# Splitting the first x load at 4 KB instead of 16 KB per partition

## Chip, cores, metric

One core of one Trainium2 chip. The metric is device time in microseconds (us); the kernel before has a median of 84.38 us (three runs, 84.36 to 84.47). All runs quoted are fast runs, with a granted clock of 1.00.

## Reference

```python
x, y: float32 [1024, 4096]
def reference(x, y, axis):          # axis = -1
    return np.sum(np.abs(x - y), axis=axis).astype(np.float32)
```

33.55 MB are read and 4 KB written. Each of the 128 partitions takes eight rows of x and y, 16 KB a row.

## The kernel before

Four rows of x go to `xa`, four of y to `yb`, the next three of x to `xb`; later rows of y reuse `yb` when VectorE has consumed it. VectorE subtracts, ScalarE takes the absolute value and sums along the row. `s_first` counts the first three transfers, each worth 16: one for each DMA engine. Every partition of a transfer is one contiguous run in memory; below, "a 16 KB row" and the like mean such a run. Each of the 16 DMA engines carries 8 of the 128. The last row is cut into five pieces.

```python
PIECES = [1728, 1024, 640, 384, 320]
...
    for r in (slice(0, 1), slice(1, H)):            # 16 KB, then 48 KB a partition
        put(lambda: nc.sync.dma_start(out=xa[:, r, :], in_=xr[:, r, :]).then_inc(s_first, 16), before="Drain")
    put(lambda: nc.scalar.dma_start(out=yb, in_=yr[:, 0:H, :]).then_inc(s_first, 16))
    put(lambda: nc.sync.dma_start(out=xb[:, 0:H - 1, :], in_=xr[:, H:K - 1, :]).then_inc(s_xb, 16))
    for k in range(H - 1):
        put(lambda: nc.sync.wait_ge(s_sub, k + 1))
        put(lambda: nc.sync.dma_start(out=yb[:, k, :], in_=yr[:, H + k, :]).then_inc(s_row[k], 16))
    ...                                             # the last row, in pieces, x and y by turns
    for k in range(H):
        sub(xa[:, k, :], yb[:, k, :], [(s_first, 48)] if k == 0 else [])
        absum(xa[:, k, :], ro[:, k:k + 1], s_act)
    sub(xb[:, 0, :], yb[:, 0, :], [(s_xb, 16), (s_row[0], 16)])     # "the fifth subtraction"
    ...
```

## Time and profile before

| | before |
|---|---|
| median time | 84.38 us |
| span in the profile | 82.8 us |
| VectorE busy, ScalarE busy | 36.4 us, 31.5 us |
| share of the 16 DMA engines' span | 95.7% |
| first subtraction starts | 41.14 us |
| idle before the fifth subtraction | 2.02 us |
| last reduction starts | 80.82 us |

The transfers fill the whole span; each compute engine is idle for over half of it. (Times of single packets in the prediction are 0.03 to 0.04 us early throughout: its first packet at 0.97 us is at 1.01 us from the start of the span, its last at 79.88 is at 79.92. Below they are counted from the start of the span.)

### The profile page before, as it was taken

The page shows a single profiled execution, that of the slowest core. Times are in us where ns is not written, and L with a number is a line of the kernel's source. Part 1 is how long each engine was busy: PE and PEld are TensorE (multiplying, and loading weights), DVE is VectorE, ACT ScalarE, POOL GpSimd, SP SyncE. Part 2 cuts the span into 40 slices and gives each one's busy share as a digit, 9 for nine tenths or more (in the row PEclk, how much of TensorE's full clock was granted, in tenths as well). Part 3 has the DMA queues.
Part 4 walks back from the last instruction along what each step waited for, and adds up shares of the span by engine and source line. Part 5 has one row for each costly group of instructions (what it writes and reads, how often), then busy time and mean ns, then how long its engine had stood idle before and what let it go on. Part 6 is the DMA issues. An engine that isn't in the chain of part 4 may idle for free.

```text
span 82.8 us, 104 instructions
## 1 busy us (share of the span) xinstructions
DVE 36.4 (44%) x16; ACT 31.5 (38%) x27; POOL 0.2 (0%) x4
## 2 busy tenths in 40 slices
DVE  0000000000000000000199999999279898999772
ACT  2400000000000000000000988979690599999990
POOL 0000000000000000000000000000000000000000
DMA  5992999989999999998888999859999999999950
GB/s 127 404 807 103 538 538 435 451 388 451 435 451 435 419 467 419 404 451 380 380 380 380 451 617 451 380 253 404 475 388 467 419 404 406 427 413 412 401 195 2
DMA packets 2592, 33.56 MB, mean 405 GB/s; under 512 B 416, under 2 KB 928, under 8 KB 1696
## 3 DMA queue, kind: packets, MB, share of 16 engines
q1 hardware_dynamic: 2448, 25.17, 72.3%
q10 hardware_dynamic: 144, 8.39, 23.4%
HBM read 33.55 MB, written 0.00 MB: 405 GB/s over the span
## 4 chain that ended last, share of the span: by engine, by line
DMA 63%; DVE 22%; SPq 10%; issue 1%
DMA yb_rows<-in_y_dram 63%; DVE xa_rows L128 21%; SPq L116 6%; SPq L119 4%; DVE last_piece L162 1%; DVE ro_sums L164 1%
## 5 line engine op out<-in xcount | busy, mean ns | idle before, releaser
L128 DVE TENSOR_TENSOR xa_rows<-xa_rows,yb_rows 128x4096 f32<-128x4096 f32 x4 | 17.4, 4420 | 41.1 <-DMA yb_rows<-in_y_dram 41.1
L133 ACT ACTIVATE xa_rows<-xa_rows 128x4096 f32<-128x4096 f32 x4 | 14.5, 3617 | 44.5 <-DVE xa_rows L128 44.5
L128 DVE TENSOR_TENSOR xb_rows<-xb_rows,yb_rows 128x2048 f32<-128x2048 f32 (+5 forms) x9 | 17.9, 2015 | 3.5 <-DMA yb_rows<-in_y_dram 3.5
L133 ACT ACTIVATE xb_rows<-xb_rows 128x2048 f32<-128x2048 f32 (+5 forms) x9 | 15.1, 1681 | 3.0 <-DVE xb_rows L128 2.9
L133 ACT ACT_TABLE_LOAD x1 | 1.3, 1283 | 1.7 <-PEq L186 1.7
L133 ACT ACTIVATION_READ_ACCUMULATOR xb_rows<-xb_rows 128x1 f32 x9 | 1.7, 186 | 0.0
L133 ACT ACTIVATION_READ_ACCUMULATOR xa_rows<-xa_rows 128x1 f32 x4 | 0.7, 186 | 0.0
L162 DVE TENSOR_TENSOR last_piece<-xb_rows,yb_rows 128x320 f32<-128x320 f32 x1 | 0.5, 492 | 0.3 <-DMA yb_rows<-in_y_dram 0.3
L164 DVE TENSOR_REDUCE ro_sums<-last_piece 128x1 f32<-128x324 f32 x1 | 0.5, 491 | 0.0
L156 DVE TENSOR_REDUCE ro_sums<-half_sums 128x2 f32<-128x4 f32 x1 | 0.1, 150 | 0.0
L186 POOL MEMSET const-bfloat16-1.0<- 128x1 bf16 x1 | 0.1, 101 | 0.0
L186 POOL MEMSET const-uint8-127<- 128x1 uint8 x1 | 0.1, 101 | 0.0
L186 POOL MEMSET const-float32-0.0<- 128x1 f32 x1 | 0.1, 98 | 0.2 <-issue 0.2
L186 POOL MEMSET const-float32-1.0<- 128x1 f32 x1 | 0.1, 98 | 0.0
## 6 DMA issues: line engine op xcount, KB each, us to landing
xa_rows<-in_x_dram SPq DMA_DIRECT2D x1, 6144.0 KB, 36.9
xb_rows<-in_x_dram SPq DMA_DIRECT2D x1, 6144.0 KB, 54.4
yb_rows<-in_y_dram SPq DMA_DIRECT2D x3, 2048.0 KB, 15.4
xa_rows<-in_x_dram SPq DMA_DIRECT2D x1, 2048.0 KB, 17.0
xb_rows<-in_x_dram SPq DMA_DIRECT2D x1, 864.0 KB, 17.7
yb_rows<-in_y_dram SPq DMA_DIRECT2D x1, 864.0 KB, 15.8
xb_rows<-in_x_dram SPq DMA_DIRECT2D x1, 512.0 KB, 16.6
yb_rows<-in_y_dram SPq DMA_DIRECT2D x1, 512.0 KB, 17.4
```

The source lines that it names most:

```text
L116: put(lambda: nc.sync.dma_start(out=xb[:, H - 1, c], in_=xr[:, K - 1, c]).then_inc(s_piece[i], 16))
L119: put(lambda: nc.sync.dma_start(out=yb[:, H - 1, c], in_=yr[:, K - 1, c]).then_inc(s_piece[i], 16))
L128: put(lambda: nc.vector.tensor_sub(out=tx, in0=tx, in1=ty).then_inc(s_sub, 1))
L133: put(lambda: nc.scalar.activation(tx, tx, ABS, accum_out=to).then_inc(sem, 1))
L156: put(lambda: nc.vector.reduce_sum(out=ro[:, K - 3:K - 1], in_=half, axis=AX).then_inc(s_end, 1))
L162: put(lambda: nc.vector.tensor_sub(out=last[:, n_part:n_part + w], in0=tx, in1=ty).then_inc(s_end, 1))
L164: put(lambda: nc.vector.reduce_sum(out=ro[:, K - 1:K], in_=last, axis=AX, apply_absolute_value=True).then_inc(s_end, 1))
L186: nc = _bacc.Bacc("TRN2", target_bir_lowering=False, num_devices=1)
```

## The change

Same bytes, same number of transfers and waits; the cut in the first 64 KB of x per partition moves from 16 to 4 KB. A smaller first transfer might get the stream going sooner.

```diff
-    for r in (slice(0, 1), slice(1, H)):
-        put(lambda: nc.sync.dma_start(out=xa[:, r, :], in_=xr[:, r, :]).then_inc(s_first, 16), before="Drain")
+    fa, fx = xa.rearrange("p k c -> p (k c)"), xr.rearrange("p k c -> p (k c)")
+    for c in (slice(0, 1024), slice(1024, H * C)):
+        put(lambda: nc.sync.dma_start(out=fa[:, c], in_=fx[:, c]).then_inc(s_first, 16), before="Drain")
```

## The prediction

> **What bounds the kernel now.** I read the page first (engine shares, the 40 slices, the DMA queues), then the waits, then the DMA view cut into stretches, and last the order in time around 58 to 66 us.
>
> ```profile
> DVE 36.4 (44%) x16; ACT 31.5 (38%) x27; POOL 0.2 (0%) x4
> ...
> DMA  5992999989999999998888999859999999999950
> ...
> q1 hardware_dynamic: 2448, 25.17, 72.3%
> q10 hardware_dynamic: 144, 8.39, 23.4%
> ```
>
> No compute engine is half busy. The two DMA queues together hold 72.3 + 23.4 = 95.7% of the 16 engines' span, which is 0.957 x 82.8 = 79.2 us. q10 is the single 8 MB load of y issued by ScalarE (128 rows of 64 KB): 0.234 x 82.8 x 16 / 128 = 2.42 us a row, or 65,536 B / 2.42 us = 27.1 GB/s an engine and 433 GB/s for sixteen. The dips in the slices (2, 5) come from counting a long packet where it starts; in the single packet records I find no engine idle between its first row at 0.97 us and the last at 79.88 us.
>
> ```profile
> DVE xa_rows L128 <- DMA yb_rows<-in_y_dram: 41.1, 1, 41.1
> DVE xb_rows L128 <- DMA yb_rows<-in_y_dram: 3.5, 6, 2.0
> ACT xb_rows L133 <- DVE xb_rows L128: 2.9, 2, 2.7
> ```
>
> VectorE starts only when one semaphore has counted three transfers: x first (16 KB a partition), x second (48 KB) and y (64 KB). The profile names y, but by the packet records the last of y's 16 counts was written at 36.9 us and the last of the second x transfer at 40.7 us, so x came last. This matters for the change. Until then 16.78 MB must land in any order; spread over their durations, the packets had moved 16.9 MB by 40.7 us. So almost nothing that is not needed was moved before the start.
>
> ```profile
> 0.00:3.00 3.00, 0.00 (x0) 1.28 (x1) 0.20 (x4) 1.00 0.72 213
> 3.00:41.00 38.00, 0.00 (x0) 0.00 (x0) 0.00 (x0) 1.00 1.03 445
> 41.00:60.50 19.50, 17.43 (x4) 13.02 (x7) 0.00 (x0) 1.00 0.95 411
> 60.50:70.00 9.50, 8.92 (x3) 6.77 (x5) 0.00 (x0) 1.00 0.98 420
> 70.00:80.00 10.00, 9.02 (x7) 9.78 (x14) 0.00 (x0) 1.00 0.99 399
> ```
>
> Last column: GB/s. Only the first 3 us are poor. A straight line through the bytes moved (3.556 MB by 10 us at 434 GB/s) meets zero at 10 - 8.19 = 1.8 us, although the first packet starts at 0.97 us: 0.83 us is lost in warming up. The first row of each engine took 0.8 to 1.68 us where later 16 KB rows take 0.611 us.
>
> ```profile
> 58.60 3.62 ACT L133 ACTIVATE xa_rows<-xa_rows 128x4096 f32<-128x4096 f32 x1 [0.62 <-DVE xa_rows L128]
> ...
> 60.59 4.42 DVE L128 TENSOR_TENSOR xb_rows<-xb_rows,yb_rows 128x4096 f32<-128x4096 f32 x1 [2.02 <-DMA yb_rows<-in_y_dram]
> ...
> 65.05 3.62 ACT L133 ACTIVATE xb_rows<-xb_rows 128x4096 f32<-128x4096 f32 x1 [2.73 <-DVE xb_rows L128]
> 65.38 2.29 DVE L128 TENSOR_TENSOR xb_rows<-xb_rows,yb_rows 128x2048 f32<-128x2048 f32 x1 [0.36 <-DMA yb_rows<-in_y_dram]
> ```
>
> Here the fifth subtraction waits 2.02 us for its row of y. The start of VectorE at 41.14 us therefore has 2.02 us of slack. Beyond it slack is short: ScalarE runs from 65.05 to 80.67 us with 0.2 us of gaps, and the last reduction, at 80.82 us, needs its sums. I put the free delay at 2.02 + 0.2 + 0.15 = about 2.35 us.
>
> **What the Trainium skill says.** "DMA: Bandwidth & Descriptors", section "Queues, rings and completion order": each DMA engine takes turns between the queues it has work for, a packet at a time. The trace agrees on the turns (16 KB x rows alternate with 64 KB y rows from about 5 us) but here a packet is one row, up to 64 KB, where the page gives 9 to 17 descriptors as typical. So the size of a row sets the share of each queue, which is what the change alters. Section "Where 436 GB/s comes from" of that page: the port ceiling is 435 GB/s. The trace shows 433 to 435 GB/s in most single microseconds from 4 us to 54 us, so the stream is at the ceiling. Section "Latency and other measured facts": a first byte comes about 0.6 us after issue on these queues; here the first row starts 0.60 us after its issuing instruction ended (0.97 against 0.376 us).
>
> **The change part by part.** The bytes, the number of DMA instructions and the number of rows (8 + 8 an engine) stay. Compute instructions and waits stay.
>
> 1. Cost a row. From 0.611 us for 16 KB and 2.418 us for 64 KB: (2.418 - 0.611) / 49,152 B gives 27.2 GB/s, and a constant of 0.611 - 16,384 / 27.2e3 = about 0.009 us. The same 16 rows pay the same constant, and the two x transfers together take 16 x 0.009 + 524,288 / 27.2e3 = 19.4 us an engine, before and after. Change: 0.0 us.
>
> 2. The start. If the first row of each engine is slow because the pipeline passes it on only when whole, a 4 KB row (0.16 us by the line above) saves 0.611 - 0.16 = 0.45 us of the 0.83 us. If it is a fixed latency, it saves nothing. I can't tell which from one size, and take a third: -0.15 us. This moves the whole stream, hence the end, one for one.
>
> 3. Running dry. The eight 4 KB rows last 8 x 0.16 = 1.3 us, so to 2.3 us or later. The second transfer is issued at 0.42 to 0.85 us, so its rows can start at 0.85 + 0.6 = 1.45 us. No gap: 0.0 us.
>
> 4. The turns. Before, y's first rows start at 4.86 to 6.12 us, after 5 to 7 rows of x. Then y gets 64 KB for each 16 or 48 KB of x and finishes first. Afterwards x rows of 60 KB face y rows of 64 KB, and both should end almost together near 40.5 us. If y starts after at most two 60 KB rows, its eighth row still goes before any row of xb (the next x load, 48 KB rows), and VectorE starts at 41.0 us as before. For each further x row that gets ahead of y's first, one xb row of 49,152 / 27.2e3 + 0.009 = 1.8 us slips in before y's last, on that engine. The semaphore waits for the slowest engine.
>
> Sum: -0.15 us with the start of VectorE unmoved, so 84.38 - 0.15 = about 84.25 us; the small chance of 4 going wrong lifts my number to 84.3 us.
>
> **The rivals.**
> (a) Faster, through a quicker first row. For: the slow first rows; the change looks made for it. Against: some engines began 0.4 us later than others, yet their second rows all start within 2.18 to 2.65 us, which looks like a latency that does not depend on the row. At best 84.38 - 0.45 = 83.9 us.
> (b) y pushed behind, so that xb rows intrude. For: y is issued at 1.26 us, and with the same 0.97 us to its first row it should have been ready at about 2.2 to 2.7 us, but it ran only 2.4 to 3.9 us later: engines had committed to some five more x rows. If they commit by number of rows, not bytes, and the 4 KB rows are over by then, five rows of 60 KB could go ahead. Against: at 2.2 to 2.7 us most of the 4 KB rows should still be in work, and they would fill that commitment. One intruding row (1.8 us) is inside the 2.35 us of slack; two (3.6 us) cost about 1.3 us: 85.6 us; three (5.4 us) cost 3.1 us: 87.4 us. A shift in order moves no bytes, so the stream would stay full and VectorE with ScalarE would become the bound.
> (c) Hidden altogether: the stream is full at both ends, nothing moves, 84.4 us. This is near my own number.
>
> **Range and chances.** Most of the weight lies between (a) at 83.9 and (c) at 84.4. I give (b) with two or more intruding rows about 15%, about half of it with three or more, which alone gives slower by 2% (above 86.07 us). Faster by 2% means 82.7 us, which would need 1.7 us off the stream; the whole warm-up is 0.83 us. So the chances are 0.01 faster, 0.92 same, 0.07 slower. The range, leaning to the slow side: 83.9 to 85.2 us.
>
> **What the profile after should show.** Step 2: the straight line through the bytes meets zero at 1.4 to 1.8 us; last row of data at 79.4 to 79.9 us. Step 3: no idle engine between 2 and 4 us. Step 4: VectorE starts between 40.6 and 43 us, and the 2 us gap before the fifth subtraction is still there or partly used. Under (b) VectorE starts at 44.5 us or later, that gap is gone, the stream still ends near 79.9 us, and the end is set by VectorE and ScalarE. The prediction would be wrong if long rows ran below 27 GB/s an engine, if an engine ran dry after its 4 KB rows, or if y waited behind many 60 KB rows.

## The result, and the profile after

84.61 us median (six runs, 84.53 to 84.88) beside 84.42 us (six runs, 84.33 to 84.58) for the kernel before. Ratio 1.0025, 95% interval 1.0008 to 1.0043. A ratio here is the mean time of one kernel's fast runs over that of the other's in the same rounds, so not quite the ratio of the medians. The loss of about 0.2 us is small but outside the noise, and the prediction had expected a gain of 0.15 us.

Waits of the changed kernel (us in total, times, longest us):

```profile
DVE xa_rows L130 <- DMA yb_rows<-in_y_dram: 42.8, 1, 42.8
DVE xb_rows L130 <- DMA yb_rows<-in_y_dram: 1.8, 5, 0.4
```

VectorE now starts 1.65 us later, and 1.7 us of its later waits are gone. In order of time (start, us), the changed kernel:

```profile
42.79 17.43 DVE L130 TENSOR_TENSOR xa_rows<-xa_rows,yb_rows 128x4096 f32<-128x4096 f32 x4 [42.79 <-DMA yb_rows<-in_y_dram]
...
60.66 4.43 DVE L130 TENSOR_TENSOR xb_rows<-xb_rows,yb_rows 128x4096 f32<-128x4096 f32 x1 [0.44 <-DMA yb_rows<-in_y_dram]
...
80.41 0.49 DVE L164 TENSOR_TENSOR last_piece<-xb_rows,yb_rows 128x320 f32<-128x320 f32 x1 [0.32 <-DMA yb_rows<-in_y_dram]
```

and the last subtraction of the kernel before:

```profile
80.29 0.49 DVE L162 TENSOR_TENSOR last_piece<-xb_rows,yb_rows 128x320 f32<-128x320 f32 x1 [0.28 <-DMA yb_rows<-in_y_dram]
```

The later start is used up in the gap before the fifth subtraction (2.02 us before, 0.44 us now). In both kernels the last subtraction waits for its transfer, so the stream still sets the end, and it comes 0.12 us later.

Why VectorE starts later is seen in the DMA view, cut to 33 to 41 us (queue, packets, MB, share; a packet is counted where it starts). q10 carries y. Kernel before:

```profile
q1 hardware_dynamic: 85, 3.39, 98.0%
q10 hardware_dynamic: 16, 0.00, 0.1%
```

Changed kernel:

```profile
q10 hardware_dynamic: 41, 2.10, 60.6%
q1 hardware_dynamic: 48, 1.77, 51.2%
```

Before, all of y's rows had started by 33 us (the last ends at 35.14 us); only its 16 counts (4-byte writes to the semaphore, one per engine) are there. Afterwards 32 of y's 128 rows are still to start. From 41.05 to 42.8 us the changed kernel shows

```profile
q1 hardware_dynamic: 16, 0.79, 103.7%
q10 hardware_dynamic: 7, 0.00, 0.2%
```

y's last data row ended at 40.83 us, but seven of its counts are written only after 41.05 us (42.22 to 42.42). Each is behind a 48 KB row of `xb` that is not needed yet: every engine had started its first one at 40.40 to 40.84 us (they are in the 33 to 41 us view), and the sixteen in this view are the second ones. The start of y's rows explains the seven. Changed kernel, 4.0 to 7.3 us and then 7.3 to 8.0 us, q10 alone:

```profile
q10 hardware_dynamic: 9, 0.59, 41.2%
```

```profile
q10 hardware_dynamic: 7, 0.46, 151.1%
```

Nine engines begin y after one 60 KB row of x (5.27 to 5.66 us), seven after two (7.47 to 7.69 us). The queues take turns, row by row, and the count takes a turn of its own. With y behind one x row: x1 y1 ... x8 y8, count of x, count of y, xb1. With y behind two: x1 x2 y1 ... x8 y7, count of x, y8, xb1, count of y. One xb row, 1.82 us, lies between the last y row and its count. The records do not name the engine, so that the seven are the same seven is inferred: from the equal numbers, here and in the runs below, and from the times, since in order of time the seven counts follow the seven starts by 34.71 to 34.76 us each, and the nine follow theirs by 35.16 to 35.19 us. The kernel before already showed the count's own turn: y's last row ended at 35.14 us, the last count came at 36.95 us, one 48 KB row of x later. There it cost nothing, as that row was needed too.

Last, the end of the stream, 79.94 to 80.2 us; kernel before, then changed kernel:

```profile
DMA packets 0, 0.00 MB, mean 0 GB/s; under 512 B 0, under 2 KB 0, under 8 KB 0
```

```profile
DMA packets 3, 0.00 MB, mean 10 GB/s; under 512 B 1, under 2 KB 3, under 8 KB 3
```

One engine is still on its last rows. The average of the 16 last counts hardly moved in this pair of profiles (79.74 before, 79.73 after); the latest of them did (79.91 before, 80.04 after).

### The profile page after: what moved, and what is told of

It reads as the page before. It is cut to its first block, busy times and chain, and to the rows that moved or that the text cites. A ratio compares the mean times of both kernels' runs of the same rounds, so it can differ in the third digit from the quotient of the medians.

```text
span 82.9 us, 104 instructions
## 1 busy us (share of the span) xinstructions
DVE 36.4 (44%) x16; ACT 31.6 (38%) x27; POOL 0.2 (0%) x4
## 4 chain that ended last, share of the span: by engine, by line
DMA 65%; DVE 22%; SPq 9%; issue 1%
DMA yb_rows<-in_y_dram 65%; DVE xa_rows L130 21%; SPq L118 6%; SPq L121 2%; DVE last_piece L164 1%; DVE ro_sums L166 1%
## 5 line engine op out<-in xcount | busy, mean ns | idle before, releaser
L130 DVE TENSOR_TENSOR xa_rows<-xa_rows,yb_rows 128x4096 f32<-128x4096 f32 x4 | 17.4, 4419 | 42.8 <-DMA yb_rows<-in_y_dram 42.8
```

What stands on the lines that cost most here:

```text
L130: put(lambda: nc.vector.tensor_sub(out=tx, in0=tx, in1=ty).then_inc(s_sub, 1))
```

## The experiments

Three questions: does the later start of VectorE cost anything, what decides when y begins, and what costs the 0.2 us? All runs compare with the kernel before on the same chip. "Last count" is when the last of the 16 engines completes the last piece of y; "mean" is the average of the 16. Both, like the two columns before them, come from the one profiled execution of each run. The span ends 2.82 to 2.90 us after the last count in every run but delay_4096 and y_after_first, where ScalarE ends later: otherwise the last count decides the time.

| run | first x load | median us | ratio (95%) | VectorE starts | gap before fifth | mean / last count |
|---|---|---|---|---|---|---|
| before | 16, 48 | 84.38 | | 41.14 | 2.02 | 79.74 / 79.91 |
| changed | 4, 60 | 84.61 | 1.0025 (1.0008 to 1.0043) | 42.79 | 0.44 | 79.73 / 80.04 |
| delay_1500 | 16, 48 | 84.37 | 1.0002 (0.9987 to 1.0017) | 42.59 | 0.39 | 79.73 / 79.85 |
| delay_4096 | 16, 48 | 86.01 | 1.0200 (1.0184 to 1.0215) | 45.46 | 0 | 79.69 / 79.94 |
| y_after_first | 4, 60 | 85.10 | 1.0073 (1.0033 to 1.0113) | 44.48 | 0 | 79.82 / 80.22 |
| x_whole | 64 | 84.46 | 1.0014 (0.9998 to 1.0031) | 42.99 | 0.23 | 79.72 / 80.03 |
| x_4_60_again | 4, 60 | 84.61 | 1.0022 (1.0006 to 1.0038) | 42.76 | 0.25 | 79.79 / 80.01 |
| x_16_48_again | 16, 48 | 84.39 | 0.9992 (0.9976 to 1.0007) | 41.05 | 2.04 | 79.65 / 79.91 |
| x_8_56 | 8, 56 | 84.45 | 1.0010 (0.9990 to 1.0030) | 41.26 | 1.90 | 79.78 / 79.96 |
| xb_in_three | 4, 60 | 84.54 | 1.0013 (0.9998 to 1.0028) | 41.89 | 1.44 | 79.77 / 80.16 |
| x_4_12_48 | 4, 12, 48 | 84.58 | 1.0032 (1.0017 to 1.0046) | 41.35 | 1.96 | 79.73 / 80.14 |
| x_1_63 | 1, 63 | 85.00 | 1.0081 (1.0058 to 1.0104) | 43.51 | 0.20 | 80.12 / 80.56 |
| x_32_32 | 32, 32 | 84.44 | 1.0017 (0.9997 to 1.0038) | 41.13 | 2.07 | 79.87 / 80.06 |

### Is the later start free?

The kernel before, with a dummy reduction in front of the first subtraction:

```diff
+    put(lambda: nc.vector.wait_ge(s_first, 48))
+    put(lambda: nc.vector.reduce_sum(out=dummy, in_=yb[:, 3, 0:1500], axis=AX))   # and 0:4096
     for k in range(H):
-        sub(xa[:, k, :], yb[:, k, :], [(s_first, 48)] if k == 0 else [])
+        sub(xa[:, k, :], yb[:, k, :], [])
```

> The kernel before, with a reduction of 1500 columns put ahead of VectorE's first subtraction: from the 0.491 us of the 324-column reduction, about 1.7 us. It delays VectorE as the change did, without touching any transfer. Theory (the stream sets the end, VectorE has about 2.35 us of slack): first subtraction at 42.8 to 42.9 us, the 2.0 us gap before the fifth falls to 0.3 us, time as before within 0.1 us. Rival (the 1.65 us later start is what costs the changed kernel its 0.2 us): the time rises by about 0.2 us.

> The same with 4096 columns, about 4.4 us. Theory: 4.4 - 2.35 = 2.1 us longer, about 86.5 us, and no gap before the fifth subtraction. Rival (slack is larger, about the 3.8 us of all VectorE gaps after its start): 0.6 us longer, 85.0 us.

delay_1500 delays the subtractions by about as much as the change did (to 42.59 us; 42.8 to 42.9 had been expected, but VectorE was released at 40.95 us here), and costs nothing: 84.37 us beside 84.37 us. The rival's 0.2 us would be a ratio of 1.0024, outside the interval. VectorE in order of time:

```profile
42.59 17.42 DVE L129 TENSOR_TENSOR xa_rows<-xa_rows,yb_rows 128x4096 f32<-128x4096 f32 x4
60.39 4.42 DVE L129 TENSOR_TENSOR xb_rows<-xb_rows,yb_rows 128x4096 f32<-128x4096 f32 x1 [0.39 <-DMA yb_rows<-in_y_dram]
```

So the later start is not the cause of the 0.2 us. delay_4096 finds where the slack ends: the subtractions start 45.46 - 41.12 = 4.34 us after VectorE was released, and the last reduction starts at 82.45 us, 1.63 us later than before.

```profile
82.45 0.49 DVE L167 TENSOR_REDUCE ro_sums<-last_piece 128x1 f32<-128x324 f32 x1 [1.64 <-ACT xb_rows L134]
```

The slack is 4.34 - 1.63 = 2.71 us; 2.35 had been estimated (hence 86.5 us expected, 86.01 measured). ScalarE, not VectorE, is the bound beyond it, as the wait in brackets says.

### How far ahead has an engine committed, and by what measure?

The changed kernel, with the 4 KB transfer on a semaphore of its own and y issued after it; and a kernel with no split at all:

```diff
 # y_after_first (s_small counts the 4 KB transfer, s_first the other two)
+    put(lambda: nc.scalar.wait_ge(s_small, 16))
     put(lambda: nc.scalar.dma_start(out=yb, in_=yr[:, 0:H, :]).then_inc(s_first, 16))
 # x_whole
-    for c in (slice(0, 1024), slice(1024, H * C)):
+    for c in (slice(0, H * C),):
```

> The changed kernel with ScalarE waiting for the 4 KB transfer before it issues y, so y is issued near 3.5 us and can be seen by the engines near 4.5 us, when the first 60 KB row is in work. Theory 1 (an engine has committed to a number of rows, about five ahead of the one in work, whatever their size): y's first rows start after six 60 KB rows, near 16.8 us; five xb rows of 1.8 us get ahead of y's last completion; VectorE starts near 50 us and the time is about 89.5 us. Theory 2 (committed by bytes, some 80 to 100 KB): y's first rows start after two or three 60 KB rows, at 7.6 to 10 us, VectorE starts at 43 to 45 us, time 84.6 to 86 us.

> The first x load in one transfer of 64 KB a partition, with the semaphore's value lowered to 32; no wait added. Theory 1 (rows counted): y's first rows start after the row in work and five more, near 16 us; four xb rows precede y's last row and a fifth its completion; VectorE starts near 50 us, time about 89.5 us. Theory 2 (bytes): y starts after two or three rows, VectorE starts at 43 to 45 us, 84.6 to 86 us. If neither holds and y starts after one row: 84.4 us, start at 41 us.

Commitment by a fixed number of rows is refuted: it asked for starts near 50 us. In x_whole y begins at 6.47 to 7.05 us on all 16 engines, after two 64 KB rows: the one in work and one more. With 16 KB rows it was five to seven, with 32 KB rows three or four (x_32_32). That fits an amount of the order of 100 KB (six rows of 16 KB are 98 KB, three of 32 KB the same, two of 64 KB 131 KB), but it is an estimate: rows are too coarse to fix it. A rival is not separated from it: a fixed time from the issue of y to its first turn. Counted from the issue (1.26 us in the kernel before, 0.78 us in x_whole, 3.92 us in y_after_first), a time of about 3.5 to 4.5 us, and then the wait for the end of the row in work, fits these runs as well; 100 KB at 27.2 GB/s last 3.7 us.

The order of turns, on the other hand, is confirmed. In x_whole (84.46 us, less than the 84.6 to 86 us of theory 2) all 16 counts of y come after one xb row (42.08 to 42.66 us, while y's data ended at 40.86 us). In y_after_first thirteen engines begin y after two x rows and three after three (9.51 to 9.78 us); thirteen counts come at 42.12 to 42.83 us, three at 43.79 to 44.05 us, one more xb row later. Then VectorE starts at 44.48 us, 3.34 us later than before, and ends beyond the slack: 3.34 - 2.71 = 0.63 us expected, and the last reduction is at 81.48 us against 80.82 us. (One of its four timed runs took only 84.43 us, the others 85.08 to 85.17; that one was not profiled.)

```profile
44.48 17.43 DVE L132 TENSOR_TENSOR xa_rows<-xa_rows,yb_rows 128x4096 f32<-128x4096 f32 x4 [44.48 <-DMA yb_rows<-in_y_dram]
...
81.48 0.49 DVE L168 TENSOR_REDUCE ro_sums<-last_piece 128x1 f32<-128x324 f32 x1 [0.46 <-ACT xb_rows L137]
```

So a rival that the prediction had feared, the late y, is real; its size stayed inside the slack in the changed kernel.

### Smaller intruding rows

```diff
-    put(lambda: nc.sync.dma_start(out=xb[:, 0:H - 1, :], in_=xr[:, H:K - 1, :]).then_inc(s_xb, 16))
+    for k in range(H - 1):
+        put(lambda: nc.sync.dma_start(out=xb[:, k, :], in_=xr[:, H + k, :]).then_inc(s_xb, 16))
 ...
-    sub(xb[:, 0, :], yb[:, 0, :], [(s_xb, 16), (s_row[0], 16)])
+    sub(xb[:, 0, :], yb[:, 0, :], [(s_xb, 48), (s_row[0], 16)])
```

> The changed kernel with the second x load (xb, 48 KB a partition) issued as three loads of 16 KB a partition. Theory (in the changed kernel one xb row gets its turn between y's last row and y's completion count): the intruding row is now 0.61 us and not 1.82 us, so VectorE starts 1.2 us earlier, near 41.6 us; the gap before the fifth subtraction grows to about 1.6 us; time as the changed kernel within 0.15 us, since the start of VectorE has slack. Rival (60 KB rows are slow in themselves): VectorE's start stays at 42.8 us.

```profile
41.89 17.43 DVE L131 TENSOR_TENSOR xa_rows<-xa_rows,yb_rows 128x4096 f32<-128x4096 f32 x4 [41.89 <-DMA yb_rows<-in_y_dram]
```

The last count of y moves from 42.42 to 41.52 us and VectorE starts 0.9 us earlier; 1.2 us had been expected. The rest is that the latest engine of this run was late anyway: its last row of y ended at 40.91 us, and the count followed 41.52 - 40.91 = 0.61 us later, the time of one 16 KB row. The gap before the fifth subtraction grew to 1.44 us and the time hardly moved (84.54 us), which again shows the start of VectorE to be free. Though it too starts with 4 KB rows, its ratio of 1.0013 is not told apart from 1.

### Is the 0.2 us real, and does it come from the small first rows?

Repeats of both kernels, and the split at 8 KB:

> The changed kernel once more, for the size of its loss and for a second sample of its start. Theory L (the 0.2 us is the lag of the DMA engine that starts last: it carries the same bytes as the others and cannot catch up, and rows of 4 KB start more unevenly): last completion of the last piece 0.3 us or more behind the mean of the 16 (0.31 in the first profile), time 84.6 us, ratio 1.002 to 1.003. Rival N (the 0.2 us was the luck of one chip and hour): ratio 0.999 to 1.001.

> The kernel before, untouched, as a control of the method and a further sample of its start. Ratio 0.999 to 1.001; lag of the last engine 0.12 to 0.25 us as in the three samples so far (0.17, 0.12, 0.25).

> Split at 8 KB. Theory on the turns (an engine has about 80 to 130 KB committed when y becomes visible near 2.5 us): y starts after one 56 KB row at most, so no xb row gets ahead of y's completion: VectorE starts at 41.0 to 41.3 us, or 42.9 if some engine takes two. Theory L: lag between those of 16 and 4 KB, time 84.4 to 84.6 us. Rival N: 84.4 us.

The loss repeats (1.0022), and the control has none (0.9992). The lag of the last engine does not separate as cleanly as expected: 0.22 us in x_4_60_again and 0.26 us in x_16_48_again. What does separate these two starts is the time of the last count: 79.85 to 79.94 us in the four runs that start with 16 KB rows (before, x_16_48_again and the two delays), 80.01 to 80.22 us in the five that start with 4 KB rows. Their averages are 79.90 and 80.11 us: 0.21 us apart, the size of the loss. About two thirds of this are the lag of the latest engine (0.20 and 0.35 us on average), the rest the mean of the 16 (79.70 and 79.77 us). But a late last count is not peculiar to small rows: x_whole has 80.03 us and x_32_32 80.06 us, with 64 and 32 KB rows. In x_8_56 all engines begin y after one 56 KB row (6.30 to 6.62 us) and all counts of y are there by 40.75 us with no xb row ahead of them. So none of 16 engines behind two rows gives no late count, seven give seven (changed), eleven give eleven (x_4_60_again), sixteen give sixteen (x_whole).

The next run starts with 4 KB rows but keeps the order of the kernel before behind them:

```diff
-    for c in (slice(0, 1024), slice(1024, H * C)):
+    for c in (slice(0, 1024), slice(1024, C), slice(C, H * C)):      # and s_first to 64
```

> First x load in three: 4, 12 and 48 KB a partition. It starts with the small rows of the changed kernel but keeps the 48 KB rows of the kernel before behind them, so y starts early enough to finish ahead of x and no xb row gets in: VectorE starts near 41.2 us. Theory L (small first rows leave one engine behind, and it stays behind): last completion of the last piece at 80.0 to 80.2 us, time 84.55 to 84.65 us. Rival O (the loss comes from the changed order of rows, through the intruding xb row): 84.4 us, last completion at 79.9 us.

```profile
60.74 4.42 DVE L130 TENSOR_TENSOR xb_rows<-xb_rows,yb_rows 128x4096 f32<-128x4096 f32 x1 [1.96 <-DMA yb_rows<-in_y_dram]
...
80.46 0.49 DVE L164 TENSOR_TENSOR last_piece<-xb_rows,yb_rows 128x320 f32<-128x320 f32 x1 [0.22 <-DMA yb_rows<-in_y_dram]
```

No xb row intrudes (start at 41.35 us, the gap of 1.96 us is back), and still the whole loss is there: 84.58 us, 1.0032, last count at 80.14 us. So the loss does not need the changed order of rows. A third transfer is in this run too (and y is issued 0.47 us later for it), so it isn't a pure test of the 4 KB rows; but its latest engine is 0.45 us behind the mean already when the 4 KB rows are counted, near 3 us, and 0.41 us at the end. Together with delay_1500 this makes the start of the stream the likeliest place of the loss. That small rows alone are the reason is not shown.

> First transfer of 1 KB a partition. On the turns: the eight 1 KB rows are over before y becomes visible near 2.5 us, so y starts after one or two 63 KB rows, and VectorE starts near 43 us, as with 4 KB. Theory L: lag of the last engine 0.3 us or more, 84.6 us or above. If the small first row had a use (step 2 of the prediction), the line through the bytes would meet zero earlier than the 1.82 to 1.86 us of 4 KB; a fixed latency puts it at 1.8 to 1.9 us again.

> Split at 32 KB. On the turns: at 2.5 us the first 32 KB row is in work and two or three more committed, so y starts after three or four x rows; y's last row and its completion still go ahead of any xb row, as y then faces 32 KB rows in both transfers: VectorE starts near 41.2 us. Theory L and rival N alike: 84.4 us, last completion at 79.9 to 80.0 us, zero of the line at 1.8 to 1.9 us.

These two differ from `changed` only in the cut (256 and 8192 columns). With 1 KB rows the loss grows to 0.8%. The DMA view of 79.94 to 80.6 us, where the kernel before had nothing:

```profile
DMA packets 58, 0.06 MB, mean 89 GB/s; under 512 B 12, under 2 KB 58, under 8 KB 58
```

Its line through the bytes meets zero at 2.17 us, where neither theory had it. The 1 KB rows were through in 0.04 to 0.06 us each, but the 63 KB rows behind them started at 1.52 to 2.35 us and the first of each engine took 2.80 to 3.32 us instead of the later 2.38 us. So the warm-up was not shortened; it was paid on the next row, which started later. With 32 KB the time is 84.44 us, not told apart from the kernel before (1.0017, 0.9997 to 1.0038), but the last count came at 80.06 us and not at the 79.9 to 80.0 us expected. Its stream ran at 430 GB/s between 37 and 54 us, where the kernel before has 434 and xb_in_three 432 (mean last count 79.87 us); why is open.

## Why the prediction was right or wrong

**Bound: right.** The stream sets the end in both kernels, and the time stayed within 0.3%. 84.61 us lies in the range of 83.9 to 85.2 us.

**Step 1, cost a row: right.** A 60 KB row took 2.267 us; 0.009 us and 61,440 B at 27.2 GB/s give 2.268 us.

**Step 2, the start: wrong in sign.** This is the term that was mis-sized: -0.15 us in the sum, where the whole change measured about +0.2 us. The first row did get shorter (0.16 to 0.96 us instead of 0.8 to 1.68 us), and it was worth nothing: bytes moved by 4 us (each packet spread over its time) are 0.941 MB before and 0.928 MB after, and the line meets zero at 1.78 to 1.84 us in the four runs with 16 KB rows and at 1.82 to 1.91 us in the five with 4 KB. The two signs given for this step failed: zero at 1.4 to 1.8 us (1.86 in the profile after, 1.82 on the prediction's clock) and the last row at 79.4 to 79.9 us (80.05, or 80.01). Between 4 and 64 KB the start-up loss hardly depends on the size of the row, as the argument against rival (a) suspected. Weighting that rival with a third had no ground in the trace.

What was not thought of: the semaphore at the end waits for the latest of 16 engines, and an engine hardly makes up a lag. In the changed kernel's profile the latest engine is 0.33 us behind the mean when the 4 KB rows are counted, and 0.31 to 0.32 us at the counts from 55 us to the end. It is much the same in y_after_first (0.46, then 0.40 us), xb_in_three (0.40, 0.38) and x_4_12_48 (0.45, 0.41). It is not so in x_4_60_again, the same kernel once more: 0.15 us at the start, 0.22 at the end; there the mean came late (79.79 us, 79.65 in its control x_16_48_again). And x_whole, without small rows, keeps a lag too (0.34 us at 38 us, 0.31 at the end). So the loss is measured, and the kept lag explains most of it in four of five profiles; why these starts lose more is open.

**Step 3, running dry: right** for 4 KB: no engine stopped between its 4 KB rows and its first 60 KB row, which started at 2.94 to 3.40 us. With 1 KB rows the stream does suffer there.

**Step 4, the turns: right in kind, wrong at one place.** "If y starts after at most two 60 KB rows, its eighth row still goes before any row of xb" is true, but "VectorE starts at 41.0 us as before" does not follow: the count of y needs a turn of its own, so with two rows ahead one xb row goes between row and count. Measured: 42.79 us. It stayed within the 40.6 to 43 us given for the profile after. That the time came out right in spite of this is owed to the slack, which the prediction had worked out; that it came out right in spite of step 2 is owed to how little was at stake there.

**Rival (b): its first stage happened**, one intruding row, inside the slack as it said for one row. Its fear of five 60 KB rows came from counting rows; x_whole and y_after_first refuted that. Whether bytes or time count instead is open. **The slack** was 2.71 us, not 2.35; this did not matter for the change.

## What to carry to other kernels

When a stream is full, ask what the first transfer's size can still move. Here it was only the warm-up, and none of the sizes tried, from 1 to 64 KB, beat 16 KB: the start-up loss was paid whatever the row, and with 1 KB rows it was only put off. A semaphore that counts 16 engines waits for the latest, so look at its lag and not at the mean alone. When a semaphore gathers several queues, work out the turns row by row, with the completion count as a turn of its own: a transfer that isn't needed yet can sit between the last byte and its count. Before judging a later start by a compute engine, look for the first later wait that can absorb it, and measure that slack with a dummy instruction.

## What the Trainium skill lacked or had wrong

- "DMA: Bandwidth & Descriptors", section "Queues, rings and completion order": a packet, the unit of the turns, is given as about 9 to 17 descriptors typically. Here it was one row of up to 64 KB (2.42 us) by the trace's records and by the order of turns, so long rows decide the share of each queue.
- Same section: it says that the count lands after the engine's earlier writes, but not that it takes a turn of its own among the queues. Here one 48 KB row of another queue went between the last data row (40.83 us at the latest) and the count (up to 42.42 us) on seven engines.
- No page read says how far an engine commits ahead before a newly filled queue gets its first turn. y, issued at 1.26 us, began at 4.89 to 6.15 us behind five to seven 16 KB rows; issued at 0.78 us, it began at 6.47 to 7.05 us behind two 64 KB rows.
- "DMA: Bandwidth & Descriptors", section "Latency and other measured facts": the first-byte latency agrees (about 0.6 us; 1.01 - 0.376 = 0.63 us), but a stream loses more than that at its start: the straight line through the bytes meets zero 0.8 to 0.9 us after the first packet starts (1.78 to 1.93 us against 1.0 us) with first rows of 4 to 64 KB, 1.2 us after it with 1 KB (2.17 us). The same table has a least round trip to memory of about 800 ns whatever the size, which is about as long; it does not say that a stream loses it once, and no run here shows that the two are the same.
- Same page, sections "Bandwidth" and "Rules for kernel authors": transfers of 1 MiB and more are advised, for their rate. A cost of a small first transfer at the far end of a long stream is not mentioned: the kernel with one of 0.5 MB lost 0.2% here, with the stream at 433 to 434 GB/s afterwards, and one of 8 MB gained nothing.
